# A two-layer grid diffusion block: tanh gates, interleaved score stacks, a new order of steps and two FFN tiles by Strassen

## The chip, the core and the metric

The kernel runs on one NeuronCore of a Trainium2 chip. TensorE (PE) multiplies matrices out of SBUF into PSUM, VectorE (DVE), ScalarE (ACT) and GpSimd (POOL) work on what lies in SBUF and PSUM, and DMA queues, most of them issued by SyncE (SP), move data between HBM and SBUF. Each engine runs its own instructions in the order in which they stand in the program and waits on semaphores for the others. The metric is device time in microseconds of one execution, median of several.

## What is computed

The reference is a block of two layers over 512 latent tokens (an 8 x 64 grid) and 256 context tokens, width 1024. Each layer projects the modulated input by `w_in`, runs four mixers of 256 columns each side by side, projects back by `w_out` and ends with a gated FFN of width 2816. In float32 and cut to what matters:

```python
for l in range(DEPTH):                       # 2 layers
    pl, pc = split(modulate(rms_norm(xl)) @ w_in[l]), split(modulate(rms_norm(xc)) @ w_in[l])
    ya = neighbourhood_attention(...)        # "n": windows of 8 x 16 and the context
    xb = depthwise_conv(pl[3]);  yb = rglru_bidir(xb, ...) * gelu(pl[4])      # "l"
    yc = head_rms(retention both ways) * silu(pl[8])                          # "r"
    yd = diff_output(softmax(s1) - lam * softmax(s2)) @ v                     # "d"
    xl = xl + gate * rms_norm(concat(ya, yb, yc, yd) @ w_out[l])
    g, u = split(modulate(rms_norm(xl)) @ w_ffn_in[l])
    xl = xl + gate * rms_norm((silu(g) * u) @ w_ffn_out[l])
    # layer 0 does the same for the context xc

def rglru_coeffs(xb, w_g, b_g, lam):         # one direction of the linear recurrence
    r, i = sigmoid(xb @ w_g + b_g)           # two gates
    log_a = -8.0 * r * softplus(-lam)
    a = exp(log_a)
    u = sqrt(-expm1(2.0 * log_a)) * (i * xb) # then h[t] = a[t] * h[t-1] + u[t]
```

## The kernel before

**Precision and tiles.** Every float32 operand is split into a high and a low part in the rounded format `float32r`; `mm3` (line 652) makes one product of three matmuls (high by high, high by low, low by high). Activations lie transposed, 128 features on the partitions and 512 latent (and, in layer 0, 256 context) tokens along the row, so one step of a projection is a matmul of 512 columns and one of 256. SBUF tiles come from pools `T` (26 of 128 x 1024), `D` (7 of 128 x 3072) and `t` (6 of 128 x 512); PSUM tiles are `s` (2 of 1024 columns) and `a` (4 of 512). A name such as `D_4u` in the profile is slot 4 of pool D.

**Steps and their order.** The mixers are generators that yield after each step: `steps_diff`, `steps_na`, `steps_lru`, `steps_ret` (lines 1911 to 1971), and `m`, a filler that computes modulation vectors of later use (matmuls with the tile `sT`). `mixers` (line 1972) walks along a string `ORDER[l]`, one letter a step. This gives a list of operations in program order, not yet the order on the engines: `Issue.run` (line 379) plans the program as a list scheduler, with a cost for each operation, and at each point takes for each engine the operation that can start first. Three tables steer it, one entry for each of seven phases of the program: `AHEAD` (how far in the list an operation may run ahead), `LIMIT` (how many tiles of a kind may be live) and `BIAS` (by how many ns VectorE must be earlier than ACT to get a copy that either can do). Every instruction is then issued in the planned order from one line, so the profile names line 571 throughout.

**LRU (`lru`, line 1056).** For each of two blocks of 128 channels and each direction `e`: two products into PSUM give the gates, ACT applies a Sigmoid with the bias column (128 x 768), then Exp, Tanh (`av`, `th`, from `cneg` and `cpos`), VectorE squares and combines, ACT takes a Sqrt, VectorE multiplies gate, input and root and runs the scans. In the profile the gates are `T_..<-s,cols_0u`. Exp and Tanh stand in one table of ACT's functions, Sigmoid and Sqrt in one of their own each; a change of table is the instruction ACT_TABLE_LOAD.

**Score stacks (`diff_stack`, line 1282; `diff_unit`, line 1312).** The differential attention of a block of two heads multiplies maps of 32 features. K or Q is projected, roped, split into high and low, written to the DRAM tile `dstk`, and loaded back into a D tile as a stack: for each of four maps `u` four loads' worth of rows, high or low by `w`, so that one matmul of 128 rows sums the products of high and low. Four DMAs bring a stack:

```python
big[32 * g:32 * g + 32].bitcast(F32)      # group g of 32 partitions
w = (0, 0, 1, 1)[g] if nm == "K" else g % 2
```

Each has rows of n floats (n = 768 in layer 0, 3072 bytes; 512 in layer 1 for Q). There are eight stacks: two layers, two blocks, K and Q.

**FFN (`ffn`, line 1704).** `w_ffn_in` gives 22 pairs of gate and up tiles. `ffn_pair` (line 1623) makes a pair by Strassen's scheme: seven products of four steps of three matmuls of 256 columns (in layer 1), 84 matmuls, with sums of weights and results on VectorE, GpSimd and ACT. `ffn_pair8` (line 1684) makes it plainly: two halves of the tokens, gate and up, eight steps, 96 matmuls and fewer sums. The tuple `CLASSIC[l]` holds the positions that go plainly.

Of the kernel before, what the change touches and what calls it, by code (L numbers as in the profile page):

```python
# [171 lines left out]
class Issue:  # L172
# [10 lines left out]
    AHEAD = (10 ** 9, 183, 161, 90, 339, 157, 40)  # L183
    LOCK = 1
    BIAS = (100, 800, 500, 300, 50, 300, 100)
# [14 lines left out]
    def box(self, ap, row):  # L200

        dims = [tuple(d) for d in ap.ap]
        if row is None:
            lo = ap.offset + sum(min(0, s * (n - 1)) for s, n in dims)
            return 0, 1, lo, ap.offset + sum(max(0, s * (n - 1)) for s, n in dims) + 1
        p, c = divmod(ap.offset, row)
        lo = c + sum(min(0, s * (n - 1)) for s, n in dims[1:])
        return p, p + dims[0][1], lo, c + sum(max(0, s * (n - 1)) for s, n in dims[1:]) + 1
# [13 lines left out]
    def add(self, eng, fn, a, k, alts=None):  # L222
# [6 lines left out]
        for w, v, start in self.touched(fn, a, k):  # L229
# [10 lines left out]
            hit = lambda ob: ob[0] < box[1] and box[0] < ob[1] and ob[2] < box[3] and box[2] < ob[3]  # L240
            if w:
# [332 lines left out]
class Net:  # L574
# [10 lines left out]
    CLASSIC = ((), (0, 1, 2, 6, 10, 14, 18, 21))  # L585
# [115 lines left out]
    def setup2(self):  # L701
# [8 lines left out]
        V = nc.vector  # L710
# [21 lines left out]
        V.tensor_scalar(self.cpos, p[:, 16:24], 8.0, None, ALU.mult)  # L732
        V.tensor_scalar(self.cneg, p[:, 16:24], -8.0, None, ALU.mult)
# [322 lines left out]
    def lru(self, l, hT, ctx):  # L1056
# [4 lines left out]
        for b in range(2):  # L1061
# [26 lines left out]
            for e in range(2):  # L1088
                rg, ig = self.W(nm="rg"), self.W(nm="ig")
                for g, dst in ((0, rg), (1, ig)):  # L1090
                    o = ((2 * e + g) * 2 + b) * 128
                    bc = self.cols[:, 52 + 8 * l + 4 * e + 2 * g + b:53 + 8 * l + 4 * e + 2 * g + b]
                    ps = self.S("lg")
                    for a, n in ((0, 512), (512, 256)):
                        self.mm3(ps[:, a:a + n], gwh[:, o:o + 128], gwl[:, o:o + 128], xh[:, a:a + n], xlo[:, a:a + n], True, True)
                    nc.scalar.activation(dst[:, 0:768], ps[:, 0:768], AF.Sigmoid, bias=bc)
# [4 lines left out]
                nc.scalar.activation(av[:, n], rg[:, n], AF.Exp, scale=cn)  # L1101
                nc.scalar.activation(th[:, n], rg[:, n], AF.Tanh, scale=cp)
# [3 lines left out]
                self.tt(ig[:, n], ig[:, n], xb[:, n], ALU.mult)  # L1106
                self.tt(u[:, n], th[:, n], ig[:, n], ALU.mult)
# [174 lines left out]
    def diff_stack(self, l, hT, b, ctx, nm, st):  # L1282
        nc, V = self.nc, self.nc.vector
        shuf = list(range(16, 32)) + list(range(16))
        for s in ((10,) if nm == "K" else (9,)):
# [418 lines left out]
    def ffn(self, l, B, ctx, order):  # L1704
# [19 lines left out]
        for i, f in enumerate(seq):  # L1724
            next(self.filler, None)
# [14 lines left out]
        list(self.filler)  # L1740
# [348 lines left out]
```

## Time and profile before

| what | value |
|---|---|
| median of three runs | 1724.28 us (1724.24 to 1730.76) |
| profiled execution | 1723.69 us, span 1721.8 us |
| TensorE busy | 1638.8 us, 95% |
| VectorE busy | 1245.6 us, 72% |
| ACT busy | 843.0 us, 49%, of it 44 table loads with 56.5 us |
| GpSimd busy | 171.0 us, 10% |

The program's stages along TensorE: modulation and transposes to 45 us, the mixers of layer 0 to 424, its `w_out` and FFN-in to 838, its FFN-out to 1011, the mixers of layer 1 to 1313, `w_out` and FFN-in to 1595, FFN-out to the end. A timeline row gives start and duration of an instruction, its operands, and in brackets how long the engine had idled before it and which instruction or transfer ended that; TensorE's rows overlap, since matmuls are pipelined, so the distance between starts is what one costs.

### The profile page before, as it was taken

The page shows a single profiled execution, that of the slowest core. Times are in us where ns is not written, and L with a number is a line of the kernel's source. Part 1 is how long each engine was busy: PE and PEld are TensorE (multiplying, and loading weights), DVE is VectorE, ACT ScalarE, POOL GpSimd, SP SyncE. Part 2 cuts the span into 40 slices and gives each one's busy share as a digit, 9 for nine tenths or more (in the row PEclk, how much of TensorE's full clock was granted, in tenths as well). Part 3 has the DMA queues.
Part 4 walks back from the last instruction along what each step waited for, and adds up shares of the span by engine and source line. Part 5 has one row for each costly group of instructions (what it writes and reads, how often), then busy time and mean ns, then how long its engine had stood idle before and what let it go on. Part 6 is the DMA issues. An engine that isn't in the chain of part 4 may idle for free. (4 is left out here: it accounts for less than half of the span.)

```text
span 1721.8 us, 26818 instructions
## 1 busy us (share of the span) xinstructions
PE 1638.8 (95%) x10511; PEld 1422.5 (83%) x10511; DVE 1245.6 (72%) x2115; ACT 843.0 (49%) x1387; POOL 171.0 (10%) x152
## 2 busy tenths in 40 slices
PE   7998999999989999999999889899989999999998
PEld 4887777677769999999887778778868799999886
DVE  5676755748579877887689998896766897776342
ACT  4367734767464434343444476755455544343221
POOL 1000100000111011001000230012121100111000
PEclk8999999999999999999999999999999999999999
DMA  9251477657554232232855562434134422323232
GB/s 379 107 147 62 136 235 236 223 193 262 188 207 169 79 111 92 87 116 104 313 176 192 182 223 95 122 99 120 37 112 152 171 83 102 111 96 101 98 122 86
DMA packets 81757, 255.14 MB, mean 148 GB/s; under 512 B 8676, under 2 KB 14148, under 8 KB 81632
## 3 DMA queue, kind: packets, MB, share of 16 engines
q1 hardware_dynamic: 81368, 253.33, 43.2%
q8 instruction: 82, 1.34, 0.3%
q14 instruction: 43, 0.35, 0.1%
q10 hardware_dynamic: 264, 0.11, 0.0%
HBM read 225.32 MB, written 28.08 MB: 147 GB/s over the span
## 5 line engine op out<-in xcount | busy, mean ns | idle before, releaser
L571 ACT ACT_TABLE_LOAD x44 | 56.5, 1283 | 12.9 <-PE s L571 6.9
L571 PE MATMUL s<-D_6u,D_4u 128*128 128x256 f32 (+1 forms) x65 | 18.0, 363 | 8.5 <-DMA T_11u<-in_rope_dq_dram 4.4
L571 PEld LDWEIGHTS s<-D_6u,D_4u 128*128 128x128 f32 x65 | 10.6, 188 | 15.4 <-ACT T_10u L571 4.8
L571 DVE TENSOR_TENSOR st_2u<-st_2u 128x1 f32<-128x1 f32 x2 | 0.3, 160 | 30.3 <-ACT T_11u L571 23.8
L571 PE MATMUL s<-D_4u,D_5u 128*128 128x256 f32 (+1 forms) x34 | 9.9, 374 | 9.9 <-DVE T_14u L571 5.5
L571 POOL TENSOR_TENSOR st_5u<-st_2u,mhalf_0u 128x1 f32<-128x1 f32 (+1 forms) x4 | 5.0, 1241 | 123.2 <-DVE st_2u L571 123.2
L571 PE MATMUL a<-D_3u,T_18u 128*128 128x384 f32 (+2 forms) x56 | 17.1, 340 | 0.0
L571 ACT COPY t_4u<-s 128x384 f32<-128x384 f32 (+1 forms) x10 | 4.5, 447 | 25.6 <-PE s L571 25.6
L571 PE MATMUL a<-D_2u,T_7u 128*128 128x256 f32 (+1 forms) x56 | 16.6, 323 | 0.0
L571 ACT COPY t_5u<-s 128x256 f32<-128x256 f32 (+1 forms) x15 | 6.2, 412 | 19.2 <-PE s L571 19.2
L571 PE MATMUL a<-D_3u,T_7u 128*128 128x256 f32 (+2 forms) x48 | 15.5, 337 | 0.0
L571 PEld LDWEIGHTS s<-D_4u,D_5u 128*128 128x128 f32 x34 | 5.8, 198 | 11.5 <-DVE T_14u L571 5.8
L571 PE MATMUL a<-D_3u,T_24u 128*128 128x384 f32 (+2 forms) x48 | 15.2, 344 | 0.0
L571 POOL TENSOR_TENSOR T_17u<-T_13u,T_1u 128x1024 fp32r<-128x1024 f32 x1 | 2.4, 2409 | 126.6 <-DMA T_24u<-in_w_ffn_in_dram 126.6
L571 PE MATMUL s<-D_2u,T_1u 128*128 128x256 f32 (+1 forms) x64 | 14.8, 290 | 0.0
L571 PE MATMUL a<-D_0u,T_7u 128*128 128x256 f32 (+2 forms) x44 | 14.4, 343 | 0.0
L571 ACT ACTIVATE t_5u<-t_5u 128x384 f32<-128x384 f32 (+1 forms) x13 | 6.2, 476 | 15.9 <-DVE t_5u L571 15.9
L571 PE MATMUL a<-D_3u,T_20u 128*128 128x512 f32 (+2 forms) x40 | 14.0, 349 | 0.0
L571 PE MATMUL a<-T_6u,D_3u 128*128 128x256 f32 x48 | 13.7, 286 | 0.0
L571 PE MATMUL a<-D_0u,T_12u 128*128 128x384 f32 (+2 forms) x44 | 13.6, 338 | 0.0
L571 ACT COPY t_1u<-s 128x384 f32<-128x384 f32 (+1 forms) x14 | 6.3, 448 | 14.7 <-PE s L571 14.7
L571 ACT ACTIVATE T_11u<-s 128x512 f32<-128x512 f32 x2 | 1.2, 594 | 24.3 <-PE s L571 24.3
(4179 smaller groups left out, 6756.3 us busy)
## 6 DMA issues: line engine op xcount, KB each, us to landing
T_6u<-in_w_mod_dram SPq DMA_DIRECT2D x9, 512.0 KB, 7.2
D_4u<-dstk SPq DMA_DIRECT2D x12, 384.0 KB, 8.5
T_20u<-in_w_mod_dram SPq DMA_DIRECT2D x8, 512.0 KB
T_13u<-in_w_mod_dram SPq DMA_DIRECT2D x8, 512.0 KB, 6.1
T_2u<-in_w_ffn_in_dram SPq DMA_DIRECT2D x8, 512.0 KB, 4.2
T_2u<-in_w_mod_dram SPq DMA_DIRECT2D x7, 512.0 KB
T_1u<-in_w_ffn_in_dram SPq DMA_DIRECT2D x7, 512.0 KB, 5.1
T_13u<-in_w_ffn_out_dram SPq DMA_DIRECT2D x7, 512.0 KB, 3.8
```

The lines of the kernel that those rows point to most:

```text
L571: getattr(getattr(self.real, op.eng), fn)(*map(real, a), **{x: real(v) for x, v in k.items()})
```

## The change

Gates: the Sigmoid becomes a Tanh of half the argument, with `hb`, half the bias columns, and the factors 1/2 and the added 1 go into the operations behind (a bias on the Exp and Tanh, `scalar_tensor_tensor` in place of `tensor_tensor`). Stacks: group g of a stack takes the partitions g, g+4, g+8, ..., and the planner's `box` learns such steps, so that the four loads of a stack count as disjoint. FFN: positions 6 and 10 of layer 1 leave `CLASSIC`. Order: new strings, new `LIMIT`, `AHEAD` and `BIAS` entries, other splits of the `w_out` blocks among the passes (`WCH`) and one more block kept between them in layer 1 (`RES`). `FILL` and the moved `list(self.filler)` change no instruction here: the filler is empty by then.

```diff
-    AHEAD = (10 ** 9, 183, 161, 90, 339, 157, 40)
+    AHEAD = (10 ** 9, 183, 161, 90, 339, 135, 40)
-    BIAS = (100, 800, 500, 300, 50, 300, 100)
+    BIAS = (100, 800, 500, 0, 200, 300, 200)
...
-        return p, p + dims[0][1], lo, c + sum(max(0, s * (n - 1)) for s, n in dims[1:]) + 1
+        step = max(dims[0][0] // row, 1)
+        return p, p + step * (dims[0][1] - 1) + 1, lo, c + sum(max(0, s * (n - 1)) for s, n in dims[1:]) + 1, step
...
-            hit = lambda ob: ob[0] < box[1] and box[0] < ob[1] and ob[2] < box[3] and box[2] < ob[3]
+            hit = lambda ob: (ob[0] < box[1] and box[0] < ob[1] and ob[2] < box[3] and box[2] < ob[3] and
+                              not (ob[4] == box[4] and (ob[0] - box[0]) % box[4]))
...
-    WCH = (((4, 4), (3, 1, 1, 3)), ((2, 1, 1, 1, 3), (2, 1, 1, 1, 3)))
-    RES = (2, 6)
+    WCH = (((3, 2, 1, 1, 1), (3, 1, 1, 3)), ((4, 4), (1, 1, 2, 4)))
+    RES = (2, 7)
...
-    CLASSIC = ((), (0, 1, 2, 6, 10, 14, 18, 21))
+    CLASSIC = ((), (0, 1, 2, 14, 18, 21))
...
-             "dldllldlrdllrdrdrddrrdrdldnrddnnnnnnnrnrrdnnnnrn")
+             "dlllldlrdlldrdddrdrrrddrdldnrdnnnnnnnrnrrndnnnrn")
...
-        V.tensor_scalar(self.cpos, p[:, 16:24], 8.0, None, ALU.mult)
-        V.tensor_scalar(self.cneg, p[:, 16:24], -8.0, None, ALU.mult)
+        V.tensor_scalar(self.cpos, p[:, 16:24], 4.0, None, ALU.mult)
+        V.tensor_scalar(self.cneg, p[:, 16:24], -4.0, None, ALU.mult)
+        self.hb = c.fixed([128, 16], "hb")
+        V.tensor_scalar(self.hb, self.cols[:, 52:68], 0.5, None, ALU.mult)
...
-                    nc.scalar.activation(dst[:, 0:768], ps[:, 0:768], AF.Sigmoid, bias=bc)
+                    nc.scalar.activation(dst[:, 0:768], ps[:, 0:768], AF.Tanh, bias=bc, scale=0.5)
...
-                nc.scalar.activation(av[:, n], rg[:, n], AF.Exp, scale=cn)
-                nc.scalar.activation(th[:, n], rg[:, n], AF.Tanh, scale=cp)
+                nc.scalar.activation(av[:, n], rg[:, n], AF.Exp, scale=cn, bias=cn)
+                nc.scalar.activation(th[:, n], rg[:, n], AF.Tanh, scale=cp, bias=cp)
...
-                self.tt(ig[:, n], ig[:, n], xb[:, n], ALU.mult)
-                self.tt(u[:, n], th[:, n], ig[:, n], ALU.mult)
+                V.scalar_tensor_tensor(ig[:, n], ig[:, n], 1.0, xb[:, n], ALU.add, ALU.mult)
+                V.scalar_tensor_tensor(u[:, n], th[:, n], 0.5, ig[:, n], ALU.mult, ALU.mult)
...
-                nc.sync.dma_start(big[32 * g:32 * g + 32].bitcast(F32),
+                nc.sync.dma_start(big[g::4].bitcast(F32),
```

ACT, the second LRU block of layer 0 (the stretch from 155 us): gates are the ACTIVATEs that read `s_80` or `s_81` with `cols_0u` or `hb_0u`, those with `cneg_0u` and `cpos_0u` are the Exp and the Tanh, those of a tile onto itself the Sqrt. Before:

```order
L571 ACT_TABLE_LOAD
L571 ACTIVATE T_16u_1691<-s_80,cols_0u_157 128x768
L571 ACTIVATE T_12u_1698<-s_81,cols_0u_157 128x768
L571 ACT_TABLE_LOAD
L571 ACTIVATE T_20u_1703<-T_16u_1691,cneg_0u_748 128x768
L571 ACTIVATE T_24u_1729<-T_16u_1691,cpos_0u_746 128x768
L571 ACT_TABLE_LOAD
L571 ACTIVATE T_2u_1732<-s_80,cols_0u_157 128x768
L571 ACT_TABLE_LOAD
L571 ACTIVATE T_24u_1729<-T_24u_1729 128x768
L571 ACT_TABLE_LOAD
L571 ACTIVATE T_12u_1751<-s_81,cols_0u_157 128x768
```

and now:

```order
L573 ACTIVATE T_3u_1696<-s_80,hb_0u_164 128x768
L573 ACTIVATE T_18u_1704<-T_3u_1696,cneg_0u_750 128x768
L573 ACTIVATE T_21u_1709<-s_81,hb_0u_164 128x768
L573 ACTIVATE T_20u_1713<-T_3u_1696,cpos_0u_748 128x768
L573 ACTIVATE T_0u_1723<-s_80,hb_0u_164 128x768
L573 ACT_TABLE_LOAD
L573 ACTIVATE T_20u_1713<-T_20u_1713 128x768
L573 ACT_TABLE_LOAD
L573 ACTIVATE T_20u_1742<-s_81,hb_0u_164 128x768
L573 ACTIVATE T_18u_1754<-T_0u_1723,cneg_0u_750 128x768
L573 ACTIVATE T_7u_1762<-T_0u_1723,cpos_0u_748 128x768
L573 ACT_TABLE_LOAD
```

The gates of both directions, the Exp and the Tanh stand without a table load between them, and a load remains only around each Sqrt.

PE, ahead of the first score unit of block 1 in layer 0 (`s_81<-D_6u,D_4u` begins 28 rows on in both): the end of a projection, and the start of the next. Before:

```order
L571 MATMUL a_79<-D_2u_520,T_16u_2579 128x512
L571 MATMUL a_79<-D_3u_527,T_16u_2579 128x512
L571 MATMUL a_79<-D_2u_520,T_7u_2633 128x512
L571 MATMUL a_77<-D_0u_287,T_13u_2589 128x256
L571 MATMUL a_77<-D_1u_297,T_13u_2589 128x256
L571 MATMUL a_77<-D_0u_287,T_2u_2647 128x256
```

and now:

```order
L573 MATMUL a_77<-D_3u_530,T_15u_2514 128x512
L573 MATMUL a_77<-D_2u_523,T_18u_2537 128x512
L573 MATMUL a_79<-T_11u_2454,sT_0u_147 2x512 x2
L573 MATMUL a_79<-T_7u_2467,sT_0u_147 2x512 x2
L573 MATMUL a_79<-T_6u_2483,sT_0u_147 2x512 x2
L573 MATMUL a_79<-T_3u_2494,sT_0u_147 2x512 x2
L573 MATMUL a_76<-D_0u_290,T_21u_2571 128x256
L573 MATMUL a_76<-D_1u_300,T_21u_2571 128x256
```

Eight modulation matmuls (of 2 rows, with `sT_0u`) have moved in between the two projections; before, they stand at other places of the program.

PE, the FFN of layer 1, position 6 (pair f3). Before, by `ffn_pair8`, where the up tile of the first half of the tokens ends (`s_81`) and the gate tile of the second begins (`s_80`):

```order
L571 MATMUL s_81<-D_3u_12221,T_1u_12850 128x256
L571 MATMUL s_81<-D_2u_12262,T_1u_12850 128x256
L571 MATMUL s_81<-D_3u_12221,T_11u_12869 128x256
L571 MATMUL s_80<-D_1u_12426,T_18u_12822 128x256
L571 MATMUL s_80<-D_6u_12436,T_18u_12822 128x256
L571 MATMUL s_80<-D_1u_12426,T_19u_12836 128x256
```

and now, by `ffn_pair`, where one of Strassen's products ends (`a_78`) and the next begins (`s_80`):

```order
L573 MATMUL a_78<-D_5u_12538,T_25u_12915 128x256 x2
L573 MATMUL a_78<-D_5u_12538,T_16u_12954 128x256
L573 MATMUL s_80<-D_4u_12485,T_3u_12944 128x256
L573 MATMUL s_80<-D_5u_12538,T_3u_12944 128x256
L573 MATMUL s_80<-D_4u_12485,T_21u_12969 128x256
```

The 96 matmuls of the pair have become 84, each product into a PSUM tile of its own, with weights that are sums of blocks.

## Rows read from the trace of the kernel before

**Rows 1.** The page, parts 1 and 5: busy us, share, xinstructions.
```profile
PE 1638.8 (95%) x10511; PEld 1422.5 (83%) x10511; DVE 1245.6 (72%) x2115; ACT 843.0 (49%) x1387; POOL 171.0 (10%) x152
...
L571 ACT ACT_TABLE_LOAD x44 | 56.5, 1283 | 12.9 <-PE s L571 6.9
```

**Rows 2.** Windows: us, then PE, PEld, DVE, ACT, POOL, clock, DMA, GB/s.
```profile
903.00:1011.00 108.00, 99.82 (x432) 79.99 (x430) 103.09 (x159) 51.76 (x91) 19.38 (x10) 0.97 0.55 194
...
1376.00:1591.00 215.00, 215.00 (x1831) 215.00 (x1830) 169.86 (x276) 89.84 (x138) 14.39 (x7) 1.00 0.30 99
```

**Rows 3.** PE's timeline in the FFN of layer 1: start, duration, instruction.
```profile
1502.98 0.28 PE L571 MATMUL s<-D_3u,T_4u 128*128 128x256 f32 x1
...
1504.28 0.28 PE L571 MATMUL s<-D_3u,T_15u 128*128 128x256 f32 x1
```

**Rows 4.** Groups of VectorE by shape, same FFN: busy us, mean ns.
```profile
L571 DVE TENSOR_TENSOR t_4u<-t_4u,a 128x256 f32<-128x256 f32 x5 | 2.1, 416 | 0.1
```

**Rows 5.** Timeline of 154 to 180 us; in brackets idle before, releaser.
```profile
157.58 0.90 ACT L571 ACTIVATE T_12u<-s,cols_0u 128x768 f32<-128x768 f32 x1
...
157.74 0.50 PE L571 MATMUL s<-T_13u,T_1u 128*128 128x512 f32 x1 [1.28 <-ACT T_16u L571]
...
158.49 1.28 ACT L571 ACT_TABLE_LOAD   x1
158.51 0.96 DVE L571 TENSOR_TENSOR T_12u<-T_12u,T_14u 128x768 f32<-128x768 f32 x1 [0.84 <-ACT T_12u L571]
...
160.03 0.60 PE L571 MATMUL a<-T_2u,sT_0u 128*2 128x512 f32 x2
...
160.46 0.60 PE L571 MATMUL a<-T_2u,sT_0u 128*2 128x512 f32 x2
...
163.03 0.96 DVE L571 SCALAR_TENSOR_TENSOR T_24u<-T_6u,T_24u 128x768 f32<-128x768 f32 x1
...
163.82 1.16 PE L571 MATMUL s<-T_18u,T_19u 64*128 64x128 f32 x16 [2.75 <-ACT T_2u L571]
...
165.95 0.96 DVE L571 TENSOR_TENSOR T_6u<-T_24u,T_12u 128x768 f32<-128x768 f32 x1 [1.96 <-ACT T_24u L571]
...
168.18 1.23 PE L571 MATMUL s<-T_18u,T_19u 64*128 64x128 f32 x8 [0.58 <-ACT T_12u L571]
...
174.88 0.80 PE L571 MATMUL s<-D_4u,D_5u 128*128 128x512 f32 x1 [5.47 <-DVE T_14u L571]
```

**Rows 6.** Busy time of one stretch inside it, columns as in rows 2.
```profile
165.10:178.70 13.60, 7.54 (x48) 4.69 (x46) 12.55 (x17) 10.96 (x12) 0.00 (x0) 0.50 0.14 40
```

**Rows 7.** Timeline of 118 to 130 us, ACT and PE.
```profile
121.86 1.28 ACT L571 ACT_TABLE_LOAD   x1
...
124.20 1.01 PE L571 MATMUL s<-D_4u,D_5u 128*128 128x512 f32 x2 [3.39 <-ACT T_22u L571]
```

**Rows 8.** Busy time of two stretches, columns as in rows 2.
```profile
277.00:286.00 9.00, 7.67 (x48) 6.54 (x47) 1.91 (x2) 3.55 (x4) 0.00 (x0) 1.00 0.94 222
0.00:43.00 43.00, 30.35 (x391) 20.70 (x391) 21.83 (x67) 20.96 (x43) 5.97 (x24) 0.88 0.97 378
```

**Rows 9.** The score stacks' DMA tile: time from issue to landing.
```profile
DMA to landing us min/median/max: 3.2/6.6/9.2
```

**Rows 10.** PE's timeline at the first score unit of block 1, layer 0.
```profile
286.57 0.94 PE L571 MATMUL s<-D_6u,D_4u 128*128 128x512 f32 x4 [1.90 <-DMA D_4u<-dstk]
```

**Rows 11.** PE's timeline at the first score unit of layer 1.
```profile
1096.26 1.08 PE L571 MATMUL s<-D_6u,D_4u 128*128 128x512 f32 x4 [4.44 <-DMA T_11u<-in_rope_dq_dram]
```

**Rows 12.** PE's timeline at the end of layer 1's first score block.
```profile
1178.46 0.83 PE L571 MATMUL a<-ident_0u,T_2u 128*128 128x128 f32 x4 [3.67 <-ACT T_2u L571]
```

**Rows 13.** PE's timeline in layer 1's neighbourhood units.
```profile
1287.28 0.49 PE L571 MATMUL s<-T_4u,T_20u 128*128 128x512 f32 x1 [3.24 <-DVE T_20u L571]
```

**Rows 14.** PE's timeline ahead of the FFN of layer 1.
```profile
1366.50 0.44 PE L571 MATMUL s<-ident_0u,T_13u 128*128 128x128 f32 x2 [0.80 <-DVE D_5u L571]
...
1371.16 0.50 PE L571 MATMUL s<-D_3u,T_14u 128*128 128x256 f32 x2 [1.12 <-ACT T_10u L571]
```

More of the change, by code (lines that the diff above doesn't have):

```diff
@@ L204, in box @@
             lo = ap.offset + sum(min(0, s * (n - 1)) for s, n in dims)
-            return 0, 1, lo, ap.offset + sum(max(0, s * (n - 1)) for s, n in dims) + 1
+            return 0, 1, lo, ap.offset + sum(max(0, s * (n - 1)) for s, n in dims) + 1, 1
         p, c = divmod(ap.offset, row)
         lo = c + sum(min(0, s * (n - 1)) for s, n in dims[1:])
-        return p, p + dims[0][1], lo, c + sum(max(0, s * (n - 1)) for s, n in dims[1:]) + 1
+        step = max(dims[0][0] // row, 1)
+        return p, p + step * (dims[0][1] - 1) + 1, lo, c + sum(max(0, s * (n - 1)) for s, n in dims[1:]) + 1, step
     def any(self, *alts):
@@ L251, in add @@
                             op.pre.add(o)
-                            if box[0] <= ob[0] and ob[1] <= box[1] and box[2] <= ob[2] and ob[3] <= box[3]:
+                            if box[4] == 1 and box[0] <= ob[0] and ob[1] <= box[1] and box[2] <= ob[2] and ob[3] <= box[3]:
                                 continue
@@ L578 @@
     KEEP, LATE, LEAD = 2, 2, 1
-    EARLY = 8
-    WCH = (((4, 4), (3, 1, 1, 3)), ((2, 1, 1, 1, 3), (2, 1, 1, 1, 3)))
-    RES = (2, 6)
+    EARLY, FILL = 8, 22
+    WCH = (((3, 2, 1, 1, 1), (3, 1, 1, 3)), ((4, 4), (1, 1, 2, 4)))
+    RES = (2, 7)
     HOOK = 10
@@ L588 @@
     FIRST = ((3, 0), (7, 0))
-    ORDER = ("drlmddlllrddrrnllrmdrrddrmdrlmrrmmdmdrrdlndmmmddnnnmdmnnmnddnmnnnnnmnnrmnn",
-             "dldllldlrdllrdrdrddrrdrdldnrddnnnnnnnrnrrdnnnnrn")
-    LIMIT = dict(r=(6, 61, 57, 4, 1, 19, 3), m=(14, 4, 6, 34, 8, 27, 5), wh=(15, 62, 35, 12, 31, 42, 5), fw=(4, 60, 75, 13, 43, 48, 9), fa=(11, 3, 10, 19, 21, 13, 5), W=(20, 25, 11, 17, 29, 55, 37), wo=(97, 42, 17, 26, 33, 17, 22))
+    ORDER = ("drlmddlllrddrrnllrdrmrddrmdrlmrrmmdrdrmdlndmmmddnnnmdmnnnmmdndnnnnnmnnrmnn",
+             "dlllldlrdlldrdddrdrrrddrdldnrdnnnnnnnrnrrndnnnrn")
+    LIMIT = dict(r=(2, 61, 57, 4, 1, 19, 3), m=(14, 4, 6, 33, 8, 28, 5), wh=(7, 58, 35, 12, 28, 42, 5), fw=(4, 68, 77, 14, 43, 48, 9), fa=(38, 3, 10, 19, 23, 13, 9), W=(20, 43, 11, 9, 28, 32, 41), wo=(97, 51, 25, 30, 33, 17, 9))
     def __init__(self, tc, I, out, ND=7):
@@ L1091, in lru @@
                     o = ((2 * e + g) * 2 + b) * 128
-                    bc = self.cols[:, 52 + 8 * l + 4 * e + 2 * g + b:53 + 8 * l + 4 * e + 2 * g + b]
+                    bc = self.hb[:, 8 * l + 4 * e + 2 * g + b:1 + 8 * l + 4 * e + 2 * g + b]
                     ps = self.S("lg")
@@ L1724, in ffn @@
         for i, f in enumerate(seq):
-            next(self.filler, None)
+            if i < self.FILL:
+                next(self.filler, None)
             list(jobs[i])
@@ L1739, in ffn @@
                         fT[seq[j]] = dst[seq[j]]
-        list(self.filler)
+        if not ctx:
+            list(self.filler)
         self.mark()
```

## Prediction

> **What bounds the kernel now.** I read the page's table of busy time first, then the busy time by stretches, then TensorE's timeline where it is idle. TensorE is busy 1638.8 of 1721.8 us and ACT spends 56.5 us on 44 table loads [rows 1]; so the time can only fall by fewer matmuls or by shorter gaps, and all gaps together are 83 us (1721.8 less 1638.8). The stretches say where there are none: in the FFN-in of layer 1 TensorE is busy for all of 215 us, with VectorE at 169.9 and ACT at 89.8 beside it [rows 2]. Matmuls taken out there are a gain as far as VectorE can follow. In the FFN-out of layer 0 it is the other way: VectorE is busy 103.1 of 108 us and TensorE only 99.8 [rows 2]. The gaps stand in the mixers: each row of a TensorE timeline has in brackets how long it idled and who released it, and these waits (on ACT, on VectorE, on a DMA) are what the new order and the new gates can shorten. The profiled execution took 1723.69 us, 0.6 under the median of 1724.28, and the sum is made against 1723.69.
>
> **FFN, two tiles by Strassen.** Positions 6 and 10 leave CLASSIC, so each goes from 96 matmuls of 256 columns to 84: 24 fewer. Eleven such matmuls start within 1502.98 to 1504.28, 0.118 us each [rows 3], so 24 x 0.118 = 2.8 us. What it adds, some 22 VectorE operations of 256 columns at 0.42 us [rows 4], 9 us, and 12 on ACT, lies under TensorE: 169.9 + 9 of 212 us. With that cover gone it would cost up to 9 us; there are 33 left. **-2.8, nearly sure.**
>
> **Tanh gates, block 1 of the LRU in layer 0.** Here TensorE waits 1.28, 2.75 and 0.58 us for ACT and 5.47 us for VectorE, 10.1 in all [rows 5]. Up to 174.88 the old order has seven table loads of 1.28 us, one of them ahead of nearly every gate; the new has three ahead of the same work, so ACT gains 4 x 1.28 = 5.1 us, more than the 4.6 that TensorE waits for it. But the last and largest wait is for VectorE, whose chain (scans, products, T_14u as the last) ran nearly through: it is busy 12.55 of 13.6 us [rows 6], and its own waits for ACT in the stretch were 0.84 and 1.96 us [rows 5]. An earlier ACT gives it these 2.8 us and no more. The new products are scalar_tensor_tensor in place of tensor_tensor: 0.95 us against 0.96 for the same shape [rows 5], nothing. Bounds: 0 (the waits move to VectorE whole) to -10.1 (all go); a loss is excluded, since no engine gets more to do there. **-2.8.** [...]
>
> [...]
>
> **The first block's scores (124.20).** TensorE waits 3.39 us for an Exp on ACT behind a 1.28 us load [rows 7]. The new order has fewer loads ahead (ACT some 5 us earlier) but also 18 fewer matmuls of the retention (0.17 us each between 256 and 512 columns, 3.1 us) under which TensorE hid. Bounds -3.4 to +3.1, **0**.
>
> **Interleaved score stacks.** Four loads of 384 KB make a stack, each into 32 neighbouring partitions, now into every fourth. While one stack comes in (277 to 286 us) the DMA engines are 94% busy and move 222 GB/s; in the first 43 us, with loads over all 128 partitions, they are 97% busy and move 378 [rows 8]. No row shows loads into every fourth partition. If they run at the higher rate, the 1.57 MB take 4.2 us and not 7.1 (222 GB/s): -2.9 for a stack; if interleaving changes nothing, 0; the median landing is 6.6 us [rows 9]. A stack that comes earlier is worth something only where TensorE waits for one.
> At 286.57 it waits 1.90 us for it [rows 10]. Two things cover that, each alone: the faster load, and eight modulation matmuls that the new order puts ahead (T_2u's first pass starts at 160.03, the second at 160.46, so two tiles' four matmuls take 0.86 and eight 1.7 us [rows 5]). Bounds -1.9 to 0, **-1.9**.
> At 1096.26 it waits 4.44 us for the first stack of layer 1 [rows 11] (the row names a rope table, which was issued behind the stack's loads on the same queue). By the order, about eight matmuls of 512 columns, 0.23 us each, no longer stand under this load: +1.9, against -2.9 for the load. Bounds +1.9 to -4.4, **-1.0**.
>
> [...]
>
> **The rest of the new order.** Layer 1's string is mostly rewritten, and 23 w_out blocks are loaded and split instead of 24, off the path: 0. At 1178.46 TensorE waits 3.67 us on ACT, which is stuck behind a weight tile that is loaded while a stack is [rows 12]; the new order has about 2 us less work ahead, the faster stack lets the tile in earlier: -3.7 to +2, **0**. At 1287.28 it waits 3.24 for VectorE, in the neighbourhood units of block 1 [rows 13]; those of block 0 now end earlier, but the projections of block 1 end later: -3.2 to +2, **-1.0**. At 1365 to 1371 there are four waits of 0.4 to 1.1 us, 3.3 in all, the first and the last of which are [rows 14]; 18 more matmuls (2.1 us) now stand ahead, while the same engines feed both: -3.3 to 0, **-1.0**. The FFN-out of layer 0 gets some 1,700 VectorE columns more, where VectorE is full: 0 to +2.8, **0**, since part of it lies in the 4.9 us that are free.
>
> **Sum**: -2.8 - 2.8 - 1.0 + 0 - 1.9 - 1.0 + 0 - 1.0 - 1.0 + 0 = -11.5, and 1723.69 - 11.5 = **1712.2 us**. All terms at their bad ends give 1723.69 - 2.8 + 3.1 + 1.9 + 2 + 2 + 2.8 = 1732.7; all at their good ends 1723.69 - 2.8 - 10.1 - 1.9 - 3.4 - 1.9 - 4.4 - 3.7 - 3.2 - 3.3 = 1689.
>
> **Rivals.** (a) *Only the matmuls go, the waits move on.* VectorE takes over each wait, as at 174.88, where its own wait is already the largest. Then 1723.69 - 2.8 - 1.9 (the modulation matmuls) = 1719. For it: VectorE at 12.55 of 13.6 us. Against it: 2.8 us of its waits there are plainly for ACT.
> (b) *The order frees more.* The ten us at 154 to 175 go whole, because VectorE gets its work in another order too, 1096 loses its 4.4 and the others half: 1723.69 - 2.8 - 10.1 - 1.9 - 1.9 - 4.4 - 1.7 - 1.8 - 1.6 - 1.6 = 1696. For it: all of them have both a shorter supplier and, mostly, more cover; against it: it needs all of them at once.
> (c) *Interleaving does nothing*, the rate being one of 3,072-byte pieces and not of partitions: the 1096 term is +1.9 and not -1.0, the 286 one stays: 1715.1.
> (d) *Slower: loads into every fourth partition are slower.* If a stack took twice its 6.6 us, the two stacks that TensorE already waits for would cost 13.2 us more, and the two other blocks' as much less their cover: 1723.69 - 11.5 + 2.9 + 13.2 = 1728 to 1742. It decides from a landing of about 8.5 us, 6.6 and the 1.9 that the new cover gives. Nothing in the rows speaks for it but that no such load is in them.
> (e) *The new layer-1 order makes waits of its own*, at the ends above: 1723 to 1733.
>
> **How the numbers follow.** My forecast 0.47 (1705 to 1718), (a) 0.20, (b) 0.17, (c) 0.08, (d) 0.04, (e) 0.04. A measurement of this kernel tells about 0.5%, 8.6 us, from no change: faster is below 1715.7, slower above 1732.9. Faster: 0.39 of the forecast's 0.47, all of (b), half of (c): 0.60. Slower: (d) and a little of (e): 0.05. The rest, 0.35, is the same. The range 1699 to 1722 holds the forecast, (a), (c) and half of (b), and leaves out the rest of (b), (d) and (e).
>
> **What would show it.** 30 table loads and about 18 us less ACT; TensorE busy about 2.8 us less in the FFN-in of layer 1 and still without gaps; in LRU block 1 of layer 0 a sum of waits near 4 to 7 us of which VectorE ends the last; the stack's landing near 4 us; no wait at the first score unit of block 1 in layer 0. Wrong it is if the stacks land as late as before, if VectorE gets gaps under the FFN or if the rewritten layer 1 waits at places where it did not.

## The result, and the profile after

The changed kernel took 1702.16 us (median of four, 1701.69 to 1703.97) against 1724.35 us: the ratio is 0.9864, with a 95% interval of 0.9840 to 0.9888. A second set of runs, compared with the kernel before in the same set, gave 0.9870 (0.9848 to 0.9893). The forecast was 1712.2 us in a range of 1699 to 1722: the direction and the range held, the gain was nearly twice the forecast one, 22.2 us for 11.5.

The page of the changed kernel, parts 1 and 5, to be read beside [rows 1]:

```profile
span 1700.0 us, 26804 instructions
...
PE 1638.9 (96%) x10487; PEld 1420.5 (84%) x10487; DVE 1248.2 (73%) x2133; ACT 831.3 (49%) x1388; POOL 161.8 (10%) x152
...
L573 ACT ACT_TABLE_LOAD x30 | 38.5, 1283 | 7.2 <-issue 2.6
```

There are 24 matmuls and 14 table loads fewer, as the order said. But TensorE counts as busy as long as before (1638.9 for 1638.8 us): what fell is its idle time, from 83 to 61 us. Its timeline at the places of the forecast (start, duration, operands; in brackets how long it idled before and what ended that):

```profile
119.17 0.61 PE L573 MATMUL s<-D_4u,D_5u 128*128 128x512 f32 x2 [0.63 <-ACT T_17u L573]
...
155.67 0.50 PE L573 MATMUL s<-T_0u,T_7u 128*128 128x512 f32 x1 [0.53 <-ACT T_21u L573]
157.98 1.16 PE L573 MATMUL s<-T_12u,T_23u 64*128 64x128 f32 x16 [0.99 <-ACT T_0u L573]
160.82 1.87 PE L573 MATMUL a<-T_1u,sT_0u 128*2 128x512 f32 x4 [1.68 <-DMA T_1u<-in_w_mod_dram]
167.11 1.03 PE L573 MATMUL a<-T_1u,sT_0u 128*2 128x512 f32 x4 [1.23 <-DMA T_1u<-in_w_mod_dram]
169.20 0.32 PE L573 MATMUL a<-T_12u,T_24u 128*64 128x128 f32 x1 [0.70 <-DVE T_12u L573]
...
280.65 0.92 PE L573 MATMUL s<-D_6u,D_4u 128*128 128x512 f32 x4
...
1090.18 0.94 PE L573 MATMUL s<-D_6u,D_4u 128*128 128x512 f32 x4 [1.06 <-issue]
...
1483.09 0.39 PE L573 MATMUL s<-D_4u,T_18u 128*128 128x256 f32 x1 [1.12 <-DVE t_5u L573]
```

The first score unit waits 0.63 us where it waited 3.39 [rows 7]; the second LRU block has 5.1 us of waits for the 10.1 of [rows 5], two of them new ones for a modulation weight; the first score unit of block 1 waits for nothing where it waited 1.90 [rows 10], in this profile; that of layer 1 waits 1.06 for 4.44 [rows 11]; and the last row is new, inside the FFN that had no gap worth naming. At the end of the mixers of layer 0 the changed kernel is 5.9 us ahead, at the end of that layer's FFN-in 10.1, at the end of its FFN-out 13.0, at the end of layer 1's `w_out` 22.1, at the end of its FFN-in 23.3 and at the end of the program 21.8.

One profile is one execution, and single waits differ between executions. The profile of the second set (the run a_again below, the same kernel) has the first score unit of block 1 waiting for its stack after all:

```profile
282.76 1.34 PE L573 MATMUL s<-D_6u,D_4u 128*128 128x512 f32 x4 [1.85 <-DMA D_4u<-dstk]
```

while the wait at layer 1's first score unit is 0.21 us there, not 1.06. So a change of one or two microseconds in one wait of one profile is not yet the effect of an edit.

### The profile page after: what moved, and what is told of

Same layout as the page of the kernel before. It is cut to its first block, busy times and chain, and to the rows that moved or that the text cites. A ratio compares the mean times of both kernels' runs of the same rounds, so it can differ in the third digit from the quotient of the medians.

```text
span 1700.0 us, 26804 instructions
## 1 busy us (share of the span) xinstructions
PE 1638.9 (96%) x10487; PEld 1420.5 (84%) x10487; DVE 1248.2 (73%) x2133; ACT 831.3 (49%) x1388; POOL 161.8 (10%) x152
## 5 line engine op out<-in xcount | busy, mean ns | idle before, releaser
L573 PE MATMUL a<-D_0u,T_21u 128*128 128x384 f32 (+2 forms) x88 | 27.4, 340 | 0.0
L573 PE MATMUL a<-D_0u,T_12u 128*128 128x256 f32 (+2 forms) x84 | 26.4, 337 | 0.0
L573 PE MATMUL a<-D_0u,T_25u 128*128 128x256 f32 (+2 forms) x68 | 23.5, 346 | 0.0
L573 PE MATMUL a<-D_0u,T_1u 128*128 128x256 f32 (+2 forms) x76 | 22.5, 334 | 0.0
L573 PE MATMUL a<-D_0u,T_18u 128*128 128x256 f32 (+2 forms) x64 | 19.4, 335 | 0.1
L573 PE MATMUL s<-D_6u,D_4u 128*128 128x512 f32 (+1 forms) x66 | 17.9, 355 | 1.4 <-issue 1.1
L573 PE MATMUL s<-D_4u,D_5u 128*128 128x512 f32 (+1 forms) x66 | 17.8, 358 | 1.1 <-ACT T_17u L573 0.6
L573 PEld LDWEIGHTS a<-D_0u,T_21u 128*128 128x128 f32 x88 | 16.5, 190 | 2.1 <-DVE T_16u L573 0.9
L573 ACT COPY t_4u<-s 128x384 f32<-128x384 f32 (+1 forms) x16 | 6.9, 430 | 22.2 <-PE s L573 22.1
L573 PE MATMUL a<-D_2u,T_25u 128*128 128x512 f32 (+1 forms) x52 | 17.7, 341 | 0.0
L573 PE MATMUL a<-D_3u,T_12u 128*128 128x384 f32 (+2 forms) x52 | 16.9, 351 | 0.0
L573 ACT COPY t_5u<-s 128x384 f32<-128x384 f32 (+1 forms) x12 | 5.2, 434 | 23.3 <-PE s L573 23.3
```

What stands on the lines that cost most here:

```text
L573: getattr(getattr(self.real, op.eng), fn)(*map(real, a), **{x: real(v) for x, v in k.items()})
```

## The experiments

**How single edits were kept apart.** Any edit makes the planner order the whole program anew. So in most of these kernels the planner plans one version and another one's operand or function is issued in its place, one instruction for one; the order on all engines is then that of the version that was planned, and only the table loads, which follow from the functions, differ (44 with Sigmoid gates in the kernel before, 30 with Tanh gates in the changed one). `emit` does this:

```diff
+    def emit(self, *calls):
+        # the planner keeps the operation recorded last; these are issued in its place
+        self.nc.ops[-1].sub = calls
...
-            for fn, a, k in op.a if op.fn == "group" else [(op.fn, op.a, op.k)]:
+            for eng, fn, a, k in op.sub or ((op.eng, *x) for x in (op.a if op.fn == "group" else [(op.fn, op.a, op.k)])):
```

**a_contig: the new order, loads into neighbouring partitions.**

```diff
                 nc.sync.dma_start(big[g::4].bitcast(F32),
                                   spill[w, :, 0:n].rearrange("(u p) n -> p u n", u=4))
+                self.emit(("sync", "dma_start", (big[32 * g:32 * g + 32].bitcast(F32),
+                                                 spill[w, :, 0:n].rearrange("(u p) n -> p u n", u=4)), {}))
```

> The changed kernel with its own planned order of instructions on every engine, instruction for instruction, but with the stacks loaded into 32 neighbouring partitions again (only the destination of the 32 stack loads differs). Theory P (each part pays at the place where TensorE waited for it): the stacks land about 3 us later, TensorE waits again for the first score unit of block 1 in layer 0 (about 1 to 2 us) and for that of layer 1 (1.06 becomes about 3 to 4 us), so 2 to 5 us slower than the changed kernel, near 1704 to 1707. Rival O (the new order carries the gain and its cover hides the loads either way): within 1 us of 1702.

Measured 0.9912 of before (0.9890 to 0.9934), 0.42% above the changed kernel (0.9870), 7 us. Theory P, and more than its 2 to 5 us: of the profiled run's 10.9 us most is at block 1 of layer 0.

```profile
285.61 1.62 PE L577 MATMUL s<-D_6u,D_4u 128*128 128x512 f32 x4 [6.12 <-DMA D_4u<-dstk]
```

The eight modulation matmuls of the new order still stand ahead of this unit, and it waits 6.12 us, more than the 1.90 of [rows 10], since the stretch before is through sooner. So those matmuls do not cover the wait; the faster load cuts it. It does not always remove it: with interleaved loads in the new order it is 0 in the changed kernel's profile, 1.85 in that of a_again, 2.46 in a_sigmoid (next) and 3.43 in a_oldclassic (below), against 6.12 here and 6.79 in a_both (below) with 32 neighbours.

**a_sigmoid: the new order, Sigmoid gates.** Tanh with half the argument is issued as Sigmoid, the operations behind it as they were.

```diff
                     nc.scalar.activation(dst[:, 0:768], ps[:, 0:768], AF.Tanh, bias=bc, scale=0.5)
+                    b0 = 52 + 8 * l + 4 * e + 2 * g + b
+                    self.emit(("scalar", "activation", (dst[:, 0:768], ps[:, 0:768], AF.Sigmoid), dict(bias=self.cols[:, b0:b0 + 1])))
```

> The changed kernel's order, instruction for instruction, with Sigmoid gates in place of Tanh: 44 table loads again instead of 30, everything else in place. Theory P: the four loads more in LRU block 1 of layer 0 come back as waits of TensorE for ACT (two to four us there), with some at block 0 and in layer 1: 4 to 8 us slower than the changed kernel, 1706 to 1710. Rival O: the 18 us of table loads lie under other work: within 1.5 us of 1702.

Measured 0.9957 (0.9942 to 0.9973), 0.87% above the changed kernel, 15 us: more than theory P had (4 to 8). TensorE's waits in the first 172 us, and ACT's rows where the first block's gates are:

```profile
92.51 1.28 ACT L577 ACT_TABLE_LOAD   x1
93.80 0.94 ACT L577 ACTIVATE T_13u<-T_16u,cneg_0u 128x768 f32<-128x768 f32 x1
94.65 0.82 ACT L577 CAST T_19u<-T_21u 128x768 fp32r<-128x768 f32 x1
95.48 1.28 ACT L577 ACT_TABLE_LOAD   x1
...
97.73 0.80 PE L577 MATMUL s<-T_18u,T_7u 128*128 128x512 f32 x1 [2.33 <-ACT T_3u L577]
...
125.63 1.01 PE L577 MATMUL s<-D_4u,D_5u 128*128 128x512 f32 x2 [5.34 <-ACT T_17u L577]
...
164.22 0.50 PE L577 MATMUL s<-T_0u,T_7u 128*128 128x512 f32 x1 [1.29 <-ACT T_3u L577]
168.68 0.50 PE L577 MATMUL s<-T_0u,T_7u 128*128 128x512 f32 x1 [3.14 <-ACT T_21u L577]
```

The new order sets gate, Exp and gate in turn, which with Tanh gates takes no table load (from 91.78 to 99.62 ACT has none in the changed kernel); with Sigmoid a load of 1.28 us stands between each two of these, at 92.51 and 95.48. The Tanh of `cpos_0u` behind them, at 97.57, stands between two Sigmoid gates (96.78 and 98.40) without a load, so the table in use there serves Sigmoid and Tanh both; the section on the kernel before gives Sigmoid one of its own. The waits at 97.73, 125.63, 164.22 and 168.68 are 12.1 us where the changed kernel has 1.2 (0.63 and 0.53). Three of the four are the gates' doing: a_both (below), which has Sigmoid gates in this order too, waits 2.34, 1.29 and 3.14 us at the same three instructions, and a_contig, with Tanh, 0, 0 and 0.53; a fourth such wait, 2.32 us at 1063.91 in layer 1, is 2.30 in a_both and none in a_contig. The wait at 125.63 is not shown to be: a_both has none there, and a_oldclassic (below), with Tanh gates and interleaved loads, has 4.65.

**b_inter: the old order, interleaved loads.**

```diff
                 nc.sync.dma_start(big[32 * g:32 * g + 32].bitcast(F32),
                                   spill[w, :, 0:n].rearrange("(u p) n -> p u n", u=4))
+                self.emit(("sync", "dma_start", (big[g::4].bitcast(F32),
+                                                 spill[w, :, 0:n].rearrange("(u p) n -> p u n", u=4)), {}))
```

> The kernel before with its own order, instruction for instruction, and only the stack loads interleaved by four. Theory P: the wait of 1.90 us at 286.57 goes and that of 4.44 us at 1096.26 falls by about 2.9, the weight tile behind the stack at 1178 lands earlier: 4 to 7 us faster than before, 1717 to 1720. Rival O: the load is bound by its 3072-byte pieces and not by partitions: stacks land as before, within 1 us of 1724.

Measured 0.9896 (0.9878 to 0.9914), 18 us, the largest effect of one edit and above what theory P had (4 to 7). Where it comes from, in TensorE's timeline, against [rows 7], [rows 10], [rows 11] and [rows 12]:

```profile
122.06 0.61 PE L575 MATMUL s<-D_4u,D_5u 128*128 128x512 f32 x2 [1.47 <-ACT T_22u L575]
...
282.08 0.86 PE L575 MATMUL s<-D_6u,D_4u 128*128 128x512 f32 x4
...
1087.55 0.86 PE L575 MATMUL s<-D_6u,D_4u 128*128 128x512 f32 x4
...
1164.45 0.66 PE L575 MATMUL a<-ident_0u,T_2u 128*128 128x128 f32 x4 [0.71 <-ACT T_2u L575]
```

The waits fall by 1.9, 1.9, 4.4 and 3.0 us, 11.2 in all. All kernels of the old order agree in this. In the four whose loads each stay in one half of the partitions (before, b_tanh, b_half, b_alt) the four waits are 3.39 to 4.59, 1.70 to 2.66, 3.58 to 4.64 and 2.09 to 4.34 us; in the three with interleaved loads (b_inter, b_both, b_both_classic) 1.17 to 1.70, at most 0.17, none and 0.29 to 0.83. The first and the last are waits for ACT, and ACT had waited for a weight tile that was issued behind a stack (at the first, before: the stack from 98.60 us on, the tile at 100.44). Ahead of the first one, ACT's row before:

```profile
108.83 1.06 ACT L571 CAST T_3u<-T_13u 128x1024 fp32r<-128x1024 f32 x1 [2.54 <-DMA T_13u<-in_w_in_dram]
```

and with interleaved loads, where the tile was there in time:

```profile
105.98 1.03 ACT L575 CAST T_3u<-T_13u 128x1024 fp32r<-128x1024 f32 x1
```

The other part is the clock. Six microseconds around the same instruction and behind it, before (columns as in [rows 2], the granted clock is the third number from the end):

```profile
286.00:292.00 6.00, 5.43 (x18) 4.41 (x19) 1.82 (x2) 1.92 (x4) 0.00 (x0) 0.72 1.00 399
1096.00:1102.00 6.00, 5.74 (x19) 4.71 (x20) 5.08 (x6) 2.85 (x5) 0.00 (x0) 0.72 0.09 37
1178.00:1184.00 6.00, 5.54 (x25) 5.07 (x26) 4.43 (x6) 2.16 (x5) 2.04 (x4) 0.72 0.47 152
```

and with interleaved loads:

```profile
281.50:287.50 6.00, 6.00 (x30) 4.94 (x29) 2.45 (x3) 3.00 (x5) 0.00 (x0) 1.00 1.00 358
1087.30:1093.30 6.00, 5.99 (x28) 4.60 (x26) 5.83 (x7) 5.96 (x8) 0.00 (x0) 1.00 0.57 175
1164.40:1170.40 6.00, 5.95 (x34) 5.22 (x35) 4.89 (x7) 3.29 (x7) 2.04 (x4) 1.00 0.50 153
```

Behind each of these waits the granted clock was 0.72 in the mean of the six microseconds; with the wait gone, or cut to 0.71 us, it was 1.00. The same holds behind the first wait, 0.72 from 124.20 on and, with the wait cut to 1.47 us, 1.00 from 122.06 on. The windows begin up to 0.6 us ahead of the instruction; counted from it, 20, 20 and 28 matmul records become 32, 28 and 34. By an estimate from these clocks about 6 x 0.28 = 1.7 us come back each time, 6.7 for four: with the waits 17.9, for the 15.2 us by which the profiled spans differ. So these four places carry the gain, but the sum does not close. Compared instruction by instruction, b_inter also loses about 3 us between 826 and 1006 us, and gains 1.9 at 500, where a wait for ACT falls from 2.80 to 0.88; that one is 0.91 in b_half and 0.81 in b_alt as well and so not due to the step of four.

**b_tanh: the old order, Tanh gates.** With the operations behind them as in the changed kernel.

```diff
                     nc.scalar.activation(dst[:, 0:768], ps[:, 0:768], AF.Sigmoid, bias=bc)
+                    b0 = 8 * l + 4 * e + 2 * g + b
+                    self.emit(("scalar", "activation", (dst[:, 0:768], ps[:, 0:768], AF.Tanh), dict(bias=self.hb[:, b0:b0 + 1], scale=0.5)))
```

> The kernel before with its own order, instruction for instruction, and only the gates by Tanh: 30 or so table loads instead of 44. Theory P: at 154 to 175 us the waits for ACT (4.6 us) go and the one for VectorE takes up part of them, 2.8 us net there; the Exp at 124 comes earlier, 1 to 3 us; so 4 to 7 us faster than before, 1717 to 1720. Rival O: VectorE's chain takes over all of it: within 1.5 us of 1724.

Measured 0.9994 (0.9978 to 1.0010): nothing that can be told from zero, as rival O had it, but not for its reason. The place of the forecast, VectorE first and TensorE's last wait:

```profile
154.87 0.59 DVE L575 SCALAR_TENSOR_TENSOR T_10u<-T_21u,cd_0u 64x64 f32<-64x64 f32 x2 [3.39 <-ACT T_21u L575]
...
163.00 0.96 DVE L575 TENSOR_TENSOR T_6u<-T_20u 128x768 f32<-128x768 f32 x1 [0.29 <-PE a L575]
...
165.94 0.96 DVE L575 SCALAR_TENSOR_TENSOR T_6u<-T_24u,T_12u 128x768 f32<-128x768 f32 x1 [0.91 <-ACT T_24u L575]
...
174.87 0.80 PE L575 MATMUL s<-D_4u,D_5u 128*128 128x512 f32 x1 [5.99 <-DVE T_14u L575]
```

The stretch came 2.1 us later than before (its first row, of VectorE, stood at 152.75) and ended at the same 174.87: VectorE's waits fell from 3.3 to 1.2 us, so the mechanism and nearly the size of the forecast's -2.8 are there. The other old-order profiles confirm it: from that row of VectorE to that wait of TensorE it is 22.1 us in before, b_half and b_alt and 20.0 here. That the stretch came later is not the gates' doing. The first score unit waits 4.58 us and not 3.39, since ACT waits for the weight tile behind the stack:

```profile
111.02 1.05 ACT L575 CAST T_3u<-T_13u 128x1024 fp32r<-128x1024 f32 x1 [4.61 <-DMA T_13u<-in_w_in_dram]
```

and two kernels below (b_half, b_alt) have 4.59 us at this unit with Sigmoid gates; in b_half ACT waits 4.54 us for that tile, until 111.05. So Tanh gates bring nothing at the first score unit here, and the 2.1 us at block 1 are within the interval of the time, 3.8 us faster to 1.7 slower; whether they reach the end of the program is not shown.

**b_both, a_both: the two edits together in the old order, and neither in the new one.** They hold the lines of b_inter and b_tanh, and those of a_contig and a_sigmoid.

> The kernel before with its own order, instruction for instruction, with both edits: stacks interleaved by four and gates by Tanh. Theory N (the parts do not add up: interleaving pays in any order, the Tanh gates only in an order planned for them): as with interleaving alone, 0.988 to 0.991 of before. Rival S (with the waits for the stacks gone, ACT's table loads are what TensorE waits for next, so Tanh pays now): 4 us or more below interleaving alone, 0.987 or less.

> The new order, instruction for instruction, without both edits: stacks into 32 neighbouring partitions and Sigmoid gates; what is left of the change is the order, the tables of limits and the two FFN tiles by Strassen. Theory N (the order is worth nothing without the durations it was planned for): 0.998 to 1.003 of before. Rival S (the new order is better in itself, by the cover it puts under the waits): 0.993 or less.

Measured 0.9889 (0.9868 to 0.9910) and 1.0007 (0.9996 to 1.0019): theory N both times. With the changed kernel on the same chip,

> The changed kernel unaltered, on the chip of this call, as the mark for the others. Both theories: 0.984 to 0.989 of the kernel before.

which gave 0.9870, this closes a table of ratios, each to the kernel before in the same set of runs:

| | neither | stacks interleaved | Tanh gates | both |
|---|---|---|---|---|
| old order | 1 | 0.9896 | 0.9994 | 0.9889 |
| new order, two FFN tiles by Strassen | 1.0007 | 0.9957 | 0.9912 | 0.9870 |

Within a row the two edits add up. Between the rows they do not: interleaving is worth 1.0% in the old order and 0.4 to 0.5% in the new, the Tanh gates 0.1% (not told from zero) in the old and 0.9% in the new. The new order by itself, FFN tiles included, is worth nothing.

**a_oldtables: the new kernel with the old strings and limits.** All lines of ORDER, LIMIT, AHEAD, BIAS, WCH and RES as before; the planner knows of the gates and the loads.

```diff
-    AHEAD = (10 ** 9, 183, 161, 90, 339, 135, 40)
+    AHEAD = (10 ** 9, 183, 161, 90, 339, 157, 40)
-    RES = (2, 7)
+    RES = (2, 6)
...
```

> The changed kernel with the old strings ORDER and the old AHEAD, BIAS, LIMIT, WCH and RES, planned anew by the planner, which knows of the Tanh gates and the interleaved loads: the two edits and the FFN tiles without the searched tables. Theory N (interleaving is most of the gain): 0.987 to 0.991 of before, 2 to 7 us above the changed kernel. Rival S (the searched tables are most of it): 0.994 or more.

Measured 0.9940 (0.9919 to 0.9961), at the lower bound of rival S and outside theory N: a new plan under the old tables loses about 9 us against the old plan with the same two edits (b_both) and 12 against the searched one. But that the searched tables are most of the gain does not follow, since b_both has most of it without them. A plan that knows the cheaper operations is not better for it; the old tables suit the old plan.

**a_oldclassic, b_both_classic: the FFN tiles.** `CLASSIC` is set back in the one, and set to the new value with old tables, interleaved loads and Tanh gates in the other.

```diff
-    CLASSIC = ((), (0, 1, 2, 14, 18, 21))
+    CLASSIC = ((), (0, 1, 2, 6, 10, 14, 18, 21))
```

> The changed kernel with the old tuple CLASSIC: positions 6 and 10 of layer 1's FFN made plainly again, 24 matmuls more, 22 VectorE operations fewer, planned anew (only that FFN and what stands close to it moves). Theory P (my term): 2.8 us slower than the changed kernel, 0.15%, 0.9875 to 0.990 of before, with the FFN-in of layer 1 longer by 2 to 3 us. Rival V (VectorE, at 190 of 224 us there, makes TensorE wait as much as it saves): within 1 us, 0.985 to 0.987.

> The kernel before with its old strings and tables, planned as if the gates were Sigmoid and the loads as before, but with stacks interleaved, Tanh gates and the new CLASSIC: all the change but the searched order. Theory N (the order adds little once the stacks land early): 0.986 to 0.989 of before, the changed kernel's time within 0.3%. Rival O (the order is worth 5 us or more by shorter waits in the FFN-out of layer 0 and at its border): 0.989 or more.

Measured 0.9875 (0.9853 to 0.9896) and 0.9883 (0.9864 to 0.9902). Against the changed kernel (0.9870) and b_both (0.9889) that is 0.05% each, 0.9 us, within the noise: the times do not decide between theory P and rival V. The traces say more. From a matmul ahead of these tiles to one behind them (1364.93 to 1568.14 in the changed kernel) a_oldclassic takes 0.6 us longer than the changed kernel (1.0 longer than its other profile, a_again), and b_both takes 0.5 us longer than b_both_classic; theory P had 2 to 3. And what rival V names is there in part: the wait of 1.12 us for VectorE at 1483.09 stands, with 1.05 to 1.13 us, in all five profiles of the new order with these tiles (after, a_again, a_contig, a_sigmoid, a_both) and not in a_oldclassic; b_both_classic has waits of 1.07 and 0.80 us under the FFN, for ACT and for VectorE, and b_both none. The second measurement is in theory N's range: all of the change but the searched tables is at 0.9883, so what the search adds to the two edits and the FFN tiles is 0.13 to 0.19%, less than the intervals.

**b_half, b_alt: why does interleaving help?** Both keep the old order. In b_half a load goes into every second partition of one half of SBUF; in b_alt into 32 neighbours, but the loads are issued in the order 0, 2, 1, 3.

```diff
+                self.emit(("sync", "dma_start", (big[64 * (g // 2) + g % 2:64 * (g // 2) + 64:2].bitcast(F32),
+                                                 spill[w, :, 0:n].rearrange("(u p) n -> p u n", u=4)), {}))
```

```diff
+                q = (0, 2, 1, 3)[g]
+                v = (0, 0, 1, 1)[q] if nm == "K" else q % 2
+                self.emit(("sync", "dma_start", (big[32 * q:32 * q + 32].bitcast(F32),
+                                                 spill[v, :, 0:n].rearrange("(u p) n -> p u n", u=4)), {}))
```

> The kernel before with its own order, instruction for instruction; each stack load goes into every second partition of one half of SBUF (0, 2, .. 62; 1, 3, .. 63; 64, 66, ..; 65, 67, ..) instead of 32 neighbours. Theory H (what a load gains by step four is that it reaches both halves of the partitions): no gain here, 0.997 to 1.002 of before, the wait for the stack at 286 us stays near 2 us. Rival R (any step helps, since neighbouring partitions collide): as with step four, 0.988 to 0.992, and no wait there.

> The kernel before with its own order; the four loads of a stack into 32 neighbouring partitions each, as before, but issued in the order 0, 2, 1, 3, so that loads that follow one another go to different halves of the partitions. Theory H (halves): two loads that are under way together no longer share a half, so a part of the gain of step four: 0.990 to 0.997 of before. Rival R (within one load, neighbouring partitions collide): 0.998 to 1.002.

Measured 1.0013 (1.0000 to 1.0026) and 0.9990 (0.9977 to 1.0003). From the pages' parts 6 (issues, KB each, median us from issue to landing), before, b_inter, b_half and b_alt in this order:

```profile
D_4u<-dstk SPq DMA_DIRECT2D x12, 384.0 KB, 8.5
```

```profile
D_4u<-dstk SPq DMA_DIRECT2D x12, 384.0 KB, 5.9
```

```profile
D_4u<-dstk SPq DMA_DIRECT2D x12, 384.0 KB, 8.8
```

```profile
D_4u<-dstk SPq DMA_DIRECT2D x12, 384.0 KB, 7.6
```

A step of two inside one half lands no earlier than 32 neighbours (8.8 for 8.5 us) and leaves the wait at block 1 (2.66 us):

```profile
289.55 0.94 PE L575 MATMUL s<-D_6u,D_4u 128*128 128x512 f32 x4 [2.66 <-DMA D_4u<-dstk]
```

Every fourth partition of all 128 lands 2.6 us earlier, 31% (8.5 to 5.9). So it is not a step of two between partitions that helps, and the reach over both halves is what is left; a step of four inside one half was not tried, and why the reach helps is not shown. The order of issue (b_alt) brings 0.9 us in the landing (8.5 to 7.6), as theory H has it, but nothing in the time that can be measured: 0.9990 lies in rival R's range.

## Why the prediction was right or wrong

The direction was right, and so were the places; most of the sizes were not. That the time lies in the range is in part luck: the FFN term brought a third of its size at most, while the clock, the weight tiles behind the stacks and the gates in the new order brought more than was counted. The largest step that was wrong is the first below.

- **Interleaving (-1.9 at 286 us, -1.0 at 1096 us, 0 elsewhere)** is where half of the gain was missed. The size of the load was close: I worked out 2.9 us for a stack from the DMA rates of [rows 8], and the median landing of a stack's loads into D_4u fell by 2.6 (b_inter); over all transfers with `dstk` it fell from 6.6 to 4.4, near the 4 that was to show it. What failed is the step "a stack that comes earlier is worth something only where TensorE waits for one". The stack fills the DMA engines (94% busy in [rows 8]), and weight tiles queue behind it; so the faster load also shortened the waits for ACT at 124 and 1178 us, which I had at 0, by 1.9 and 3.0 in b_inter. At 124 I had not seen the tile; at 1178 I had, and set the lost cover against it. And at 1096 I set the lost cover (+1.9) against it: in the old order, without that loss, the whole 4.4 went. In the new order interleaving is worth 7 to 9 us and not 18.
- **The clock after a wait** I counted once, at 178 us, as the third term of the sum (-1.0, and -1.9 in the sum of the good ends and in rival (b)). No run shows this term; what the runs showed is a granted clock of 0.72 over six microseconds behind four waits of the kernel before and of 1.00 at the same four places in b_inter, where by the estimate above about 1.7 us come back each time. At 178 us itself the clock was at 0.50 for 13.6 us [rows 6], and in the changed kernel's profile it is 0.90 in the mean over that block (155.67 to 172.00); how much time this gave back, no run separates. The rows to see it by were there in the trace before; the clock column has to be read behind each wait.
- **Two covers at 286 us, each alone**: wrong for the matmuls (6.12 us in a_contig), right for the load in the old order (no wait in b_inter); in the new order it takes the wait from over 6 us down to between 0 and 3.43 us.
- **Tanh gates, -2.8 at block 1**: the mechanism held, 2.1 us of VectorE's own waits went in the old order. (The two products that I compared take 0.96 us both in [rows 5]; that one takes 0.95 is in no row.) That the edit's sum is not told from 0 there and is 15 us in the new order I did not see: I priced the loads that go, not an order that sets gates and Exps in turn because they no longer cost a load. This gain stands behind the "order" terms of my sum. At the first score unit, which I had at 0, 3.39 became 0.63, but no run ties that to the gates: in the new order a_both waits for nothing there without Tanh, and a_oldclassic 4.65 us with it.
- **FFN, -2.8, "nearly sure"**: mis-sized, it is -0.5 to -1.0. From the end of `w_out` to the end of the FFN-in the stretch is 235.2 us before and 234.0 after; of these 1.2 us 0.6 lie ahead of the first FFN matmul (1371.16 before, 1348.51 after). Undoing the tiles moved the time by 0.9 us, within the noise, and the stretch by 0.6 to 1.0.

```profile
1359.50:1594.70 235.20, 231.62 (x1961) 230.28 (x1961) 184.07 (x297) 100.90 (x158) 18.98 (x11) 1.00 0.31 104
```

```profile
1337.40:1571.40 234.00, 229.95 (x1937) 228.15 (x1937) 197.32 (x323) 108.06 (x168) 12.84 (x9) 1.00 0.32 106
```

  The 24 matmuls are gone (1961 to 1937 records), but TensorE's busy time fell by 1.7 us and its idle time rose by 0.5, with a wait of 1.12 for VectorE at 1483. VectorE got 13 us and not 9 (184.1 to 197.3), while GpSimd's work fell by 6 (19.0 to 12.8). So of 24 x 0.118 us 1.7 went out of the busy time, and a new wait took more of it back; why not the whole 2.8 left the busy time is open.
- **The rest**: at 1178 the wait is gone (-3.7, I had 0); at 1287 it is gone (-3.2, I had -1.0); ahead of the FFN of layer 1 the 0.6 us above went, of a forecast 1.0; the FFN-out of layer 0 became 2.9 us shorter where I had 0 with a bound on the bad side.
- **The signs.** The 30 table loads came, but ACT is busy 11.7 us less (843.0 to 831.3) and not 18. The waits at the second LRU block, 5.1 us with VectorE's as the last, are as forecast. Two of the signs of being wrong showed, both small: the wait for VectorE under the FFN, and a new wait for ACT in layer 1, 2.01 us at 1248.73 (0.87 in a_again).
- **The rivals.** (b), "the order frees more", was nearest in time and wrong in its cause: the order alone frees nothing (a_both). (a), that VectorE takes over each wait, comes near the Tanh gates in the old order, though the 2.1 us at block 1 speak against it. (c) and (d), about the loads, fell with b_inter.

What stays open: how much the searched tables are worth beside the edits (the intervals of 0.9870 and 0.9883 overlap), whether the 2.1 us that the Tanh gates save at block 1 in the old order reach the end, and what decides whether the first score unit of the new order waits 0 or 5 us. No kernel here is faster than the changed one by more than the measurement tells.

## What to carry to other kernels

Price a load that fills the DMA engines (94% busy here) by everything that queues behind it, also where the profile names another engine as the one waited for: here two waits for ACT fell by 1.9 and 3.0 us with the faster load (b_inter). Read the granted clock in the microseconds behind each wait of TensorE (0.72 over six of them, four times in the kernel before) and add what it costs to the wait's price. And when an edit comes together with a new order, price the edit in both orders: here the same two edits were worth 18 and 1 us in the one and 7 to 9 and 15 to 16 in the other, by orders that were equally fast without them. And before a single wait is explained, look for it in a second profile of the same kernel, or of one that differs elsewhere.

## What the runs showed of the hardware

- Loads of 384 KB into 32 partitions land 31% earlier when the partitions are spread over all 128 (8.5 to 5.9 us), and not at all earlier when they are spread over one half (8.8).
- After waits of 1.9 to 4.4 us the granted clock was 0.72 over the next 6 us, four times (before); with these waits gone or cut to 1.47 and 0.71 us (b_inter), it was 1.00.
- An Exp with both scale and bias from columns takes a little longer than with the scale alone. The changed kernel, and a_sigmoid in the same place:

```profile
92.72 1.03 ACT L573 ACTIVATE T_13u<-T_16u,cneg_0u 128x768 f32<-128x768 f32 x1
```

  1.03 us for the 0.94 of the row at 93.80 above, 0.09 us for each of 16 operations.
